# Two layers of a spatial-gating and attention mixer: the first queries of each attention turned later, and the second layer's first gating norm moved behind a GELU

## The chip, the cores and the metric

The kernel runs on one core of one Trainium2 chip. The metric is the device time of one execution in microseconds (us), lower is better. The time before is the median of three runs.

## The reference, cut to what matters

Two layers work on 256 latent tokens and 256 context tokens of width 2048, all in float32. Each layer normalises its input, scales and shifts it by a modulation computed from `c` and `c_ctx`, and multiplies it by one wide matrix whose columns are `u`, `v` and `za` of a gating branch and `q`, `k`, `v` and `zb` of an attention branch:

```python
u = gelu(u); v = rms_norm(gelu(v).reshape(b, n // 128, 128, 8, 128), v_norm_w)
s = einsum('gpq,bcqgd->bcpgd', w_sgu, v) + b_sgu.T[:, :, None]
sgu = u * s                                           # gating branch (SGU)
q = axial_rope(rms_norm(split_heads(q, 8), q_norm_w)) # 8 query heads, 2 key heads
p = softmax(einsum('bgrqd,bgkd->bgrqk', q, k) * 128 ** -0.5)
attn = einsum('bgrqk,bgkd->bgrqd', p, v)
y = concatenate([sgu * silu(za), attn * silu(zb)], -1) @ w_out
x = x + gate * y
```

In the first layer both token streams go through all of it; in the second the context gives only keys and values. Latent queries attend to all 512 keys, context queries to the 256 context keys.

## The kernel before, in words

Every matrix product is made of three float32r matmuls: an operand is split into a rounded high half (a copy on ScalarE, ACT) and the low half that is left (a subtraction on VectorE, DVE), and `three` multiplies high by high, low by high and high by low. L199 and L202 split a piece of weights (256 rows by 512 columns, a DMA of 512 KB into one of six `raw` buffers); `evac_split` (L474 and L475) splits what a transpose left in PSUM: keys `kT`, queries `qT`, probabilities `pt`.

The order of work on TensorE (PE), ACT, DVE and the DMA queue of SyncE (SP) is the order in which the Python program emits it, and each engine takes its own list in that order. The main stream (`Stream`) is a list of jobs, each a product with 512 weight columns. A job has eight pieces, and a piece has four **units** in the first layer (two or four in the second) of 1.3 to 1.5 us of matmuls each. After each unit `tick()` lets every waiting task emit its next step; tasks are taken in the order in which they were started, and a task's `yield n` means that it goes on n units later. `later(0, f)` emits f in the same tick, behind all older tasks.

Three tasks matter here.

- `attention_task`: it normalises and rotates keys and the first two blocks of queries, then turns (transposes on PE) the first queries (`turn_queries`, L519), splits them one unit later, and one unit after that begins its loop over heads (32 in the first layer, 16 in the second). A head's scores are in its first unit; its probabilities are turned one unit later and split one or two units after that, together with the next queries if the head is the second of its pair. `HEAD_PACE` makes a head three units long in the first layer and four in the second. No head begins while `zone[0]` is set, in the last piece of a job (four units in the first layer, two in the second). With the first head of each block of four another block's queries are normalised in the first layer (`Q_AT`), with the second in the second.
- `mod_rest`: the modulation rows that are needed later are computed as dot products on DVE (L283), two instructions a step in the first two parts and one in the last, a step every `MOD_PACE` units. It stands still while `hold[0]` is set; an attention sets it at its start and clears it just ahead of its first scores. While it stands still three `raw` buffers hold its rows.
- `head_norm` for the gating branch: after a tile's GELU has left PSUM (`sgu_v`, L659) four squares with sums on ACT (L440), a sum and a power (L427 on DVE, L428 on GpSimd, POOL), and the product (L452, DVE). `sgu_task` multiplies the tiles by the position matrices on PE (L685) `SGU_LAG` units after the job's end: 15 in the first layer, 6 in the second.

In this document h0, h1, ... are the heads of an attention. S0, S1, ... are the stream's units in the first layer from its first (32 to a job; S60 to S63 is the last piece of the job for the first half of `u`, and S64 begins the job for `za`). T1, T2, ... are the units of the second layer from the first after the key and value job: T1 to T16 is its first `v` job, T15 and T16 end its two tiles, and T17 begins the job for `u`. In the kernel before, the first layer's first queries are turned after S2, split after S3 and scored after S4; its heads begin after S4, S7, ..., S25, and then, behind each job's last piece, after S32, S35, ..., S59, and S64 and so on. In the second layer the same three steps come after T19, T20 and T21.

Lines of the helpers: L338 to L340 are the three matmuls of `three`, L533 the maximum of a head's scores on DVE, L536 its exponential on ACT, L641 the product of `u` with the gating sums on DVE, L543 the turn of the probabilities.

Of the kernel before, what the change touches and what calls it, by code (L numbers as in the profile page):

```python
# [31 lines left out]
QT_AT = 1  # L32
KEY_LAG = (3, 3)
Q_LAG = (0, 0)
NORM_PACE = (1, 1)
ACT_NORM = 'k'
ACT_SUM = 'kqs'
# [11 lines left out]
SGU_GAP = {4: 2, 2: 3}  # L49
# [3 lines left out]
WAVE = ((2, 6), 8, 10)  # L53
MOD_LOADS = ((4, 5, 6, 9), (2, 4, 6, 9))
AHEAD = {'raww': 3, 'rawm': 3}
MOD_PACE = (2.0, 1.6, 2.4)
PRE_HOLD = (True, True)
HEAD_PACE = (((1, 1, 1), (1, 1, 1), (1, 1, 1)), ((1, 2, 1),))
LAT = (0, 1)
# [3 lines left out]
def mixer_kernel(ctx: ExitStack, tc: tile.TileContext, a, out):  # L63
# [29 lines left out]
    def misc(s="ms"):  # L93
        return msp.tile([P, 512], F32, tag="ms", name=nm(s))
# [11 lines left out]
    def view(ap, pat, **kw):  # L106
        return ap.rearrange(pat, **kw)
# [202 lines left out]
    def spawn(gen, wait=0):  # L310
        tasks.append([gen, wait])
# [122 lines left out]
    def head_norm(q, n, kind):  # L434
# [3 lines left out]
        if kind in ACT_SUM:  # L438
            for h in range(n):
                S.activation(sq[:, h * HD:(h + 1) * HD], q[:, h, :], AF.Square, accum_out=ss[:, h:h + 1])  # L440
            yield NORM_PACE[0]
        else:
            S.activation(view(sq, "p (h d) -> p h d", h=n), q, AF.Square)
            yield NORM_PACE[0]
            V.tensor_reduce(out=ss, in_=view(sq, "p (h d) -> p h d", h=n), axis=AX.X, op=ALU.add)
        r = rstd_of(ss, n, HD)
        yield NORM_PACE[1]
        if kind in ACT_NORM:
# [28 lines left out]
    def attention_task(L, kv, qa, units, done):  # L477
# [20 lines left out]
        def query(u):  # L498
            hf, tt = u
            yield from norm_rope(L, "q", qa[hf][:, tt], 4, tt)  # L500
            yield Q_LAG[L["l"]]
            ready.add(u)
# [12 lines left out]
        def turn_queries(hf, tt, pr):  # L515
            assert (hf, tt) in ready
            ps = misc("qt")
            for i in range(2):
                T.transpose(out=ps[:, i * P:(i + 1) * P], in_=qa[hf][:, tt, 2 * pr + i, :], identity=ident)  # L519
            qT = t2([P, 2, 2, P], "qT", F32R)  # L520
            qT = [qT[:, 0], qT[:, 1]]
            return ps, qT
# [38 lines left out]

        while len(nk) < NT or units[0] not in ready:
            yield 1
        ps, qT = turn_queries(*pairs[0])
        yield 1
        evac_split(qT[0], qT[1], view(ps[:, :256], "p (h d) -> p h d", h=2))
        yield 1
        hold[0] = False
        paces = HEAD_PACE[L["l"]]
        n = len(heads)  # L570
# [84 lines left out]
    def sgu_v(L, buf, hf, nt):  # L655

        def f(tt, ps):
            b = buf[:, tt]
            S.activation(b, view(ps, "p (g d) -> p g d", g=4), AF.Gelu_apprx_tanh)  # L659
            spawn(head_norm(b, 4, "s"), SGU_GAP[nt] * tt)  # L660
        return f

    def sgu_consts(l, hf):
# [557 lines left out]
```

## Time and profile before

| what | before |
|---|---|
| median of 3 runs | 1194.63 us (1194.54 to 1194.81) |
| profiled execution, its own time | 1195.92 us |
| its span, first to last instruction | 1194.2 us |
| mean granted TensorE clock | 0.998 |
| PE busy, share of the span | 1163.5 us, 97% |
| DVE busy | 908.4 us, 76% |
| ACT busy | 521.8 us, 44% |
| DMA, mean over the span | 207 GB/s |

The profile is of one execution on the chip. A matmul's printed end is modelled and matmuls overlap: one of 512 columns is printed with 0.39 us and the next begins 0.23 us after it, one of 256 with 0.28 us and 0.12 us. So where the profile prints idle time ahead of a matmul, PE's issue stood still for 0.16 us longer than that.

### The profile page before, as it was taken

Reading aid. Unit: us, or ns where it says so; the run is one execution under the profiler, and the core shown is the slowest. Engines: PE = TensorE matmul, PEld = TensorE weight load, DVE = VectorE, ACT = ScalarE, POOL = GpSimd, SP = SyncE. Lnnn points to the kernel's source line nnn. Section 1 sums busy time; section 2 is a strip of 40 time slices with the busy share of each in tenths; the row PEclk is TensorE's granted clock in tenths of the full one; section 3 lists DMA queues with packets and bytes.
Section 4 is the critical chain, followed back from the end, with each engine's and each line's share of the span. In section 5 each row is a group of like instructions: output and inputs, shape, how many; then the busy total and the mean of one; then the engine's idle time right before and its main releaser. Section 6 shows DMA issues by size and latency. Waiting matters only on the chain.

```text
span 1194.2 us, 17949 instructions
## 1 busy us (share of the span) xinstructions
PE 1163.5 (97%) x6624; PEld 990.8 (83%) x6624; DVE 908.4 (76%) x1939; ACT 521.8 (44%) x992; POOL 46.9 (4%) x47
## 2 busy tenths in 40 slices
PE   4899999999999999999999999999999999999998
PEld 2567667888888888888888888987888989999998
DVE  5666769778888777989988998678558687767544
ACT  4422225565565432242232122246366777645332
POOL 0000002001000000010100000000011000000000
PEclk9999999999999999999999999999999999999999
DMA  9978672545354656676886765646456667677662
GB/s 319 372 269 303 243 267 96 158 138 181 108 160 141 191 182 208 203 233 217 264 282 211 228 200 186 229 124 218 135 164 197 218 195 222 206 260 249 223 204 89
DMA packets 131913, 247.52 MB, mean 207 GB/s; under 512 B 8641, under 2 KB 19425, under 8 KB 131825
## 3 DMA queue, kind: packets, MB, share of 16 engines
q1 hardware_dynamic: 130640, 242.08, 62.6%
q0 software_dynamic: 1184, 4.29, 1.1%
q8 instruction: 52, 0.85, 0.3%
q14 instruction: 37, 0.30, 0.1%
HBM read 244.23 MB, written 2.11 MB: 206 GB/s over the span
## 4 chain that ended last, share of the span: by engine, by line
PE 85%; DVE 6%; ACT 3%; DMA 3%; issue 1%; POOL 1%; SPq 1%; ACTq 0%; POOLq 0%; DVEq 0%
PE acc L338 25%; PE acc L340 25%; PE acc L339 25%; PE mod L231 2%; DVE lo L202 2%; DMA raw<-in_w_in 1%; DMA mod<-in_w_mod 1%; PE tp L543 1%; ACT hi L199 1%; PE sg L685 1%; DVE qa L872 1%; PE s L340 1%; PE o L339 1%; POOL rs L428 1%; PE o L340 1%
## 5 line engine op out<-in xcount | busy, mean ns | idle before, releaser
L199 ACT CAST hi<-raw 128x1024 fp32r<-128x1024 f32 (+1 forms) x242 | 250.7, 1036 | 399.8 <-PE acc L339 279.5
L202 DVE TENSOR_TENSOR lo<-raw,hi 128x1024 fp32r<-128x1024 f32 (+1 forms) x242 | 292.1, 1208 | 131.7 <-ACT hi L199 131.4
L283 DVE SCALAR_TENSOR_TENSOR junk<-raw,scb 128x512 f32<-128x512 f32 x448 | 308.0, 688 | 15.1 <-DMA raw<-in_w_modt 6.2
L338 PE MATMUL acc<-hh,hi 128*128 128x512 f32 x384 | 152.6, 397 | 0.0
L340 PE MATMUL acc<-hh,lo 128*128 128x512 f32 x384 | 149.8, 390 | 0.0
L339 PE MATMUL acc<-hl,hi 128*128 128x512 f32 x384 | 149.8, 390 | 0.0
L338 PE MATMUL acc<-hi,hh 128*128 128x512 f32 x320 | 130.2, 407 | 6.6 <-ACT hh L719 5.6
L340 PE MATMUL acc<-hi,hl 128*128 128x512 f32 x320 | 126.3, 395 | 0.1
L339 PE MATMUL acc<-lo,hh 128*128 128x512 f32 x320 | 126.3, 395 | 0.0
L338 PE MATMUL acc<-h,hi 128*128 128x256 f32 x384 | 110.3, 287 | 1.0 <-ACT s L659 1.0
L340 PE MATMUL acc<-h,lo 128*128 128x256 f32 x384 | 108.6, 283 | 0.0
L339 PE MATMUL acc<-h,hi 128*128 128x256 f32 x384 | 108.5, 283 | 0.0
L338 PE MATMUL acc<-mh,hi 128*128 128x512 f32 (+1 forms) x304 | 106.5, 350 | 0.0
L340 PE MATMUL acc<-mh,lo 128*128 128x512 f32 (+1 forms) x304 | 106.4, 350 | 0.0
L339 PE MATMUL acc<-ml,hi 128*128 128x512 f32 (+1 forms) x304 | 106.4, 350 | 0.0
L338 PEld LDWEIGHTS acc<-hi,hh 128*128 128x128 f32 x320 | 60.7, 190 | 32.3 <-issue 7.1
L340 PEld LDWEIGHTS acc<-hh,lo 128*128 128x128 f32 x384 | 72.1, 188 | 15.3
L339 PEld LDWEIGHTS acc<-hl,hi 128*128 128x128 f32 x384 | 72.3, 188 | 13.5
L338 PEld LDWEIGHTS acc<-hh,hi 128*128 128x128 f32 x384 | 72.2, 188 | 13.5
L428 POOL TENSOR_TENSOR rs<-rs,nhalf 128x4 f32<-128x4 f32 (+1 forms) x36 | 41.4, 1149 | 892.1 <-DVE rs L427 892.1
L339 PE MATMUL acc<-lo,h 128*128 128x512 f32 x192 | 75.3, 392 | 0.7 <-DVE lo L202 0.3
L338 PE MATMUL acc<-hi,h 128*128 128x512 f32 x192 | 75.7, 394 | 0.0
(163 smaller groups left out, 2158.0 us busy)
## 6 DMA issues: line engine op xcount, KB each, us to landing
raw<-in_w_in SPq DMA_DIRECT2D x173, 512.0 KB, 4.3
raw<-in_w_modt SPq DMA_DIRECT2D x128, 512.0 KB, 4.7
raw<-in_w_out SPq DMA_DIRECT2D x64, 512.0 KB, 5.0
mod<-in_w_mod SPq DMA_DIRECT2D x15, 1024.0 KB, 8.7
raw<-in_w_mod SPq DMA_DIRECT2D x30, 512.0 KB, 9.7
scb<-crow SPq DMA_DIRECT2D x12, 512.0 KB, 5.9
xT<-in_xT SPq DMA_DIRECT2D x8, 512.0 KB, 8.1
x<-in_xT POOLq DMA_DIRECT2D x4, 1024.0 KB, 11.0
```

The lines of the kernel that those rows point to most:

```text
L199: S.copy(hi, rs)
L202: V.tensor_tensor(out=lo, in0=rs, in1=hi.bitcast(F32), op=ALU.subtract)
L231: T.matmul(self.ps[j:j + 32, :wd], sc[:, k, :], self.raw[k], start=k < 4, stop=k >= KT - 4)
L283: V.scalar_tensor_tensor(out=junk, in0=rs[i][:, b_, :], scalar=1.0, in1=scbs[q][:, s_, :], op0=ALU.mult, op1=ALU.mult, accum_out=part[:, 2 ...
L338: T.matmul(ps, lhi, rhi, start=first, stop=False)
L339: T.matmul(ps, lhi, rlo, start=False, stop=False)
L340: T.matmul(ps, llo, rhi, start=False, stop=last)
L428: G.tensor_tensor(out=r, in0=r, in1=nhalf[:, :n], op=ALU.pow)
L543: T.transpose(out=tp[:, c * P:(c + 1) * P], in_=p_[:, c * P:(c + 1) * P], identity=ident)
L685: T.matmul(ps[:, tt * P:(tt + 1) * P], buf[:, tt, g, :], ws[:, g, :], start=True, stop=True)
L872: later(0, lambda: V.tensor_tensor(out=dst[:, tt], in0=ps, in1=dst[:, tt], op=ALU.add))
```

## The change

In both layers the attention waits two more units before it turns its first queries (`ENTRY`), and one unit more between their split and the first scores (`FIRST_LO`), so that the clearing of `hold[0]` and every head follow three units later than before, where the job's last piece doesn't stop them. In the second layer the norm of a `v` job's first tile starts two units later and that of the second one unit later (`SGU_AFTER`; for four tiles, the first layer, nothing changes). The three paces of `mod_rest` become 1.95, 1.55 and 2.3 units.

```diff
@@ -32,6 +32,9 @@
 Q_LAG = (0, 0)
+ENTRY = (2, 2)
+FIRST_LO = 1
+SGU_AFTER = {4: 0, 2: 2}
 NORM_PACE = (1, 1)
@@ -53,7 +56,7 @@
-MOD_PACE = (2.0, 1.6, 2.4)
+MOD_PACE = (1.95, 1.55, 2.3)
@@ -561,10 +564,11 @@
         while len(nk) < NT or units[0] not in ready:
             yield 1
+        yield ENTRY[L["l"]]
         ps, qT = turn_queries(*pairs[0])
         yield 1
         evac_split(qT[0], qT[1], view(ps[:, :256], "p (h d) -> p h d", h=2))
-        yield 1
+        yield 1 + FIRST_LO
         hold[0] = False
@@ -657,7 +661,7 @@
             S.activation(b, view(ps, "p (g d) -> p g d", g=4), AF.Gelu_apprx_tanh)
-            spawn(head_norm(b, 4, "s"), SGU_GAP[nt] * tt)
+            spawn(head_norm(b, 4, "s"), SGU_AFTER[nt] + (SGU_GAP[nt] - SGU_AFTER[nt] // 2) * tt)
         return f
```

## Rows read from the trace of the kernel before

**Rows 1.** The page, busy time: engine, us, share of the span, instructions.
```profile
PE 1163.5 (97%) x6624; PEld 990.8 (83%) x6624; DVE 908.4 (76%) x1939; ACT 521.8 (44%) x992; POOL 46.9 (4%) x47
```
**Rows 2.** Waits of PE: who, for whom, us in total, times, longest.
```profile
PE qt L519 <- DVE rs L427: 1.8, 1, 1.8
PE s L340 <- DVE qT L475: 1.4, 3, 0.8
PE acc L338 <- ACT s L659: 1.0, 1, 1.0
...
PE o L339 <- DVE pt L475: 0.3, 1, 0.3
```
**Rows 3.** Timeline, first layer's first queries: start, duration, engine, instruction [idle before].
```profile
206.19 0.69 DVE L471 TENSOR_TENSOR qa<-qa,sq 128x512 f32<-128x512 f32 x1
...
207.03 0.41 PE L519 MATMUL qt<-ident,qa 128*128 128x128 f32 x2 [1.78 <-DVE rs L427]
...
208.99 0.69 DVE L452 TENSOR_TENSOR qa<-qa,rs 128x512 f32<-128x512 f32 x1 [0.23 <-POOL rs L428]
...
210.39 0.42 DVE L475 TENSOR_TENSOR qT<-qt,qT 128x256 fp32r<-128x256 f32 x1
...
210.87 0.50 PE L340 MATMUL s<-kT,qT 128*128 128x512 f32 x1 [0.20 <-DVE qT L475]
...
212.65 1.21 DVE L202 TENSOR_TENSOR lo<-raw,hi 128x1024 fp32r<-128x1024 f32 x1
```
**Rows 4.** Timeline of PE, second layer's entry.
```profile
904.60 0.39 PE L338 MATMUL acc<-h,hi 128*128 128x256 f32 x1 [0.98 <-ACT s L659]
...
911.35 0.50 PE L340 MATMUL s<-kT,qT 128*128 128x512 f32 x1 [0.76 <-DVE qT L475]
...
914.57 0.61 PE L685 MATMUL sg<-ws,s 128*128 128x128 f32 x4
```
**Rows 5.** Timeline of ACT, the same stretch.
```profile
902.80 0.30 ACT L440 ACTIVATE sq<-s 128x128 f32<-128x128 f32 x1
...
903.97 0.58 ACT L659 ACTIVATE s<-acc 128x512 f32<-128x512 f32 x1
```
**Rows 6.** Timeline of DVE, the same stretch.
```profile
904.29 0.69 DVE L452 TENSOR_TENSOR qa<-qa,rs 128x512 f32<-128x512 f32 x1
...
912.55 0.69 DVE L452 TENSOR_TENSOR s<-s,rs 128x512 f32<-128x512 f32 x1
```
**Rows 7.** The power on POOL there: count, shortest, median, longest ns.
```profile
L428 POOL TENSOR_TENSOR rs<-rs,nhalf x4: 1006/1008/1424, 894.8 to 911.5; 128x4 f32<-128x4 f32 x4
```
**Rows 8.** Timelines of ACT, DVE and PE, first layer, S57 to S67.
```profile
311.58 0.30 ACT L440 ACTIVATE sq<-qa 128x128 f32<-128x128 f32 x1
...
315.19 0.69 DVE L533 TENSOR_REDUCE nmx<-s 128x1 f32<-128x512 f32 x1 [1.37 <-PE s L340]
...
317.65 1.28 ACT L636 ACT_TABLE_LOAD   x1
...
323.21 0.39 PE L338 MATMUL s<-kT,qT 128*128 128x512 f32 x1
...
327.31 0.68 DVE L533 TENSOR_REDUCE nmx<-s 128x1 f32<-128x512 f32 x1
...
328.43 0.39 PE L338 MATMUL s<-kT,qT 128*128 128x512 f32 x1
...
330.66 0.69 DVE L475 TENSOR_TENSOR pt<-tp,pt 128x512 fp32r<-128x512 f32 x1 [0.19 <-ACT pt L474]
```
**Rows 9.** Groups of DVE from 315.1 to 331.3: count, busy us, mean ns.
```profile
L283 DVE SCALAR_TENSOR_TENSOR junk<-raw,scb 128x512 f32<-128x512 f32 x8 | 5.5, 686 | 0.1
L641 DVE TENSOR_TENSOR s<-s,act 128x512 f32<-128x512 f32 x4 | 2.7, 684 | 0.0
```
**Rows 10.** Windows: stretch, length, busy time of PE, PEld, DVE, ACT, POOL, PEclk, DMA.
```profile
52.60:56.00 3.40, 1.32 (x6) 0.64 (x5) 3.22 (x8) 0.91 (x2) 0.00 (x0) 1.00 1.05 389
56.00:59.50 3.50, 3.50 (x10) 2.48 (x8) 3.32 (x7) 1.84 (x3) 0.00 (x0) 0.51 0.83 304
```

## Prediction

> **What bounds the kernel now.** I read the page's busy times first: PE works through 97% of the span, DVE through 76%, ACT through 44% [rows 1]. So time is to be had only where PE stands still. The list of PE's waits says where that is: behind the start of the program there are few places, and four of them belong to this change [rows 2]. The timelines then show what is late at each place; the share of DVE over the whole span hides that DVE is full at just these places. All idle times below are printed ones plus 0.16 us, because a matmul is printed 0.16 us longer than it holds up the next.
>
> **The entry of the first layer.** PE waits 1.78 us ahead of the first query turn, because the rotation of these queries (L471) begins on DVE only at 206.19, and 0.20 us more in the first scores for the split's low half [rows 3]. With 0.16 each that is 2.30 us. Two more units ahead of the turn are 2.7 us of matmuls, so the turn would be reached at 207.03 - 1.94 + 2.7 = 207.8, behind the rotation's end at 206.88: the first wait goes. What is late next is the split. Its low half now comes behind all that DVE has been given by then: the second block's product, its rotation, and a weight piece (L202) that before lay behind the scores. DVE's list doesn't move with PE there, because it waits only for the power that ends at 208.95. From the product at 208.99: product 0.7, two small products 0.7, rotation 0.7 and 0.6, weight piece 1.15, split 0.42, so 213.3 [rows 3]. PE reaches the third matmul of the scores at 207.8 + 3.0 (two units as before) + 1.4 (one more) + 0.46 = 212.7, and waits about 0.7. Gain: 2.30 - 0.72 = 1.6 us. Bounds: no new wait 2.3, a wait of 1.2 leaves 1.1.
>
> **The entry of the second layer.** Two waits [rows 4]: 0.98 for PSUM that a tile's GELU frees, 0.76 for the split; with 0.16 each 2.07 us. ACT does four squares of the first tile (902.80 on, 1.17 us for four) ahead of the second GELU at 903.97 [rows 5]. With the norm two units later this GELU begins at 902.80 and ends at 903.4, when PE wants the space (904.60 - 1.14 = 903.46): the first wait goes. Three more units hide the split. But the second tile's norm now comes one unit later, while PE is 2 us early. DVE from 904.29 [rows 6]: queries' product 0.6, weight piece 1.15, rotation 0.8, sum 0.1, rotation 1.4, first tile's product 0.65, weight piece 1.15, sum 0.1, weight piece 1.15, split 0.35, product of the second tile 0.7. That is 8.1 us, so 912.4, or 912.8 if a power takes 1.42 us and not 1.01 [rows 7]. The gating matmuls (L685), at 914.57 before [rows 4], would be reached at 914.57 - 2.07 - 0.8 (the scores now come behind them) = 911.7 and wait 0.7 to 1.2. I take 1.0; before, the product was over at 913.24 [rows 6], well ahead of them. Gain 1.1 us; bounds 0.3 and 2.07.
>
> **The heads behind the entry.** In the first layer seven heads and not eight fit ahead of S28, so behind each job's last piece another head of the pair stands: h7, h17 and h27 (second of a pair) after S32, S64 and S96, where h8, h18 and h28 (first) stood. A second head turns the next pair's queries, splits them one unit on, and the next scores need them one unit after that. The other waits in the trace go with this: one for a split at 274.8 (1.4 - 0.20 - 0.76 = 0.44 of the third row), one for a split of probabilities (0.3) [rows 2]. With 0.16 each 1.1 us.
>
> What comes in their place I worked out at S64. Before, DVE is full there: 15.5 us from the maximum after S59 (315.19) to the split after S66 (330.66), and the maximum of the scores after S64 (PE 323.21) is taken only at 327.31 [rows 8]. In the list are eight L283, four products of `u`, two weight pieces [rows 9], a rotation of queries whose squares begin at 311.58 [rows 8], and splits. It did no harm, because after S64 stood a first head: the queries of the next scores had been split ahead of the last piece. With a second head there, PE turns the next queries after S65, and their split after S66 is behind the whole list, with the scores of h18 one unit later, at about 328.7 (328.43 before [rows 8]). The list changes so: the query block belongs to h16, now after S59 and not S56, so its squares come behind the first GELU of the job's end, its product and rotation between the products of `u`. Less work by 0.8 us (no query split in between, narrower probabilities). More waits on DVE: weight piece 0.5 (ACT takes the exponential and the weights' high half 0.7 later), first product of `u` 0.75 (behind the ACT table load of 1.28 [rows 8]), probabilities 1.3 (their high half lies behind four squares and a GELU), the queries' product 0.65 (power 1.0 [rows 7]). From 315.9, where the maximum of h16 would begin: 15.5 - 0.8 + 3.2 = 17.9, so the split begins at 333.8 and ends at 334.2. The third matmul of h18's scores is due at 329.15: a wait of 5.0 us. Without any of the added waits it is 1.8. I take 4.4, since the two longest follow from ACT's order and the others may shrink.
>
> The same reckoning at S34 and S98, where no rotation or fewer sums fall into the list, leaves margins of a microsecond and more. In the second layer the queries of h6 and h14 are split right behind the last activations of a job too, but DVE has one L283 a step there and is not behind: margins of 0.2 to 0.3 us, for which I set 0.3 of loss in all, 0 to 1.
>
> **The rest.** The paces: 448 L283 as before. The first part has 64 steps, so it gains 3.2 units and starts two or three later: the sum is nothing, and around S57 to S67 its steps fall on the same units as before. The second part ends some 6 units earlier; nothing of PE waits for it [rows 2]. SP's queue: during the longer hold weights keep three of the six `raw` buffers, and each load, with all that is queued behind it on SP, waits for the L202 of the piece three earlier. By the lists above DVE's pieces come no later than before, so I cost this at nothing. If a piece were a unit late, one wait of up to 1.4 us would show at L338 behind a `lo`. No DMA is added.
>
> **Sum**, in the profiled execution (span 1194.2, its own time 1195.92, 1.29 above the median): -1.6 - 1.1 - 1.1 + 4.4 + 0.3 = +0.9 us. With 1.8 at S67 it is -1.7, with 5.0 +1.5. On the median 1194.63 that is 1195.5, own range 1192.9 to 1196.5. Other medians lie within 0.27 us, so 0.2% (2.4 us) is about the least that I call a difference.
>
> **Rivals.** (1) *Nothing new waits after S66*: DVE isn't that late, and the split is ready a unit after it is emitted. For it: in the trace queries turned behind a second head wait at only a few places [rows 2]. Against it: DVE's maximum after S64 lies 3.6 us behind PE [rows 8]. It decides below a wait of 1.1 us. Then -1.6 - 1.1 - 1.1 + 0.3 = -3.5 or, if also the gating matmuls don't wait, -4.5: 1190 to 1191.
>
> (2) *The wait after S66 slows PE's clock*, on the other side. Between 52.6 and 56.0 PE had 1.32 us of work, and in the next 3.5 us the granted clock was 0.51, the lower level (1.2 GHz of 2.4) [rows 10]. At half the rate such a stretch loses 1.7 us of work. With 5.0 us of standing at S67, broken only by two matmuls, the same can follow: +1.5 + 1.7 = 3.2, so 1197.8. It decides at a wait of about 4 us. Against it: the mean granted clock is 0.998 over the span, so the 1.94 us ahead of the first query turn had no such sequel.
> The Trainium skill, "TensorE: Matmul & The Clock Gate", section "Why this matters for your kernels", advises against gaps in TensorE's work amid a kernel for this reason: the clock falls back. By it a gap as at S67 would cost more than itself, +3.2 in place of +1.5; the dip in the trace agrees.
>
> (3) *The change doesn't do what it says*: DVE is the limit at both entries, and the waits only move. Then the gains are the lower bounds, 1.1 and 0.3: 1196.5 to 1198 with the wait at S67. I count it half to the forecast and half to (2).
>
> **Chances.** Forecast within 0.2%: 0.43. Rival (1), faster: 0.30. Slower, by (2) or the worse half of (3): 0.27. The range from 1190.6 to 1198.0 reaches into both.
>
> **What would show it.** Right: no idle PE ahead of L519 near 207; 0.5 to 1 us in the first scores; in the second layer no wait of L338 for L659, but one of about 1 us at the first L685 for L452; no wait of L340 for `qT` near 274; a wait of 3 to 5 us for `qT` in the scores after S67, near 330, with L470 and L641 ahead of the split on DVE. Wrong: if that wait is under 1 us, the kernel is faster and my order of DVE's list or its waits there are wrong; if PEclk falls near 335, rival (2).

## The result and the profile after

The changed kernel takes 1203.84 us (median of 4 runs, 1203.55 to 1204.18) against 1194.72 us of the kernel before in the same series: a ratio of 1.007, 95% interval 1.0058 to 1.0082, or 9.1 us more. The forecast was 1195.5 us with a range up to 1198.0, so the result lies 8 us over it and outside its range. The profiled execution took 1203.86 us, with a span of 1202.1 us, 7.9 us longer than that of before.

The page's busy times of the changed kernel look as before [rows 1]; the list of PE's waits doesn't (columns: us in total, times, longest):

```profile
PE 1166.9 (97%) x6624; PEld 992.4 (83%) x6624; DVE 909.8 (76%) x1939; ACT 521.5 (43%) x992; POOL 46.3 (4%) x47
```
```profile
PE s L341 <- ACT qT L477: 3.5, 1, 3.5
PE sg L689 <- DVE s L455: 1.6, 2, 0.9
PE s L343 <- DVE qT L478: 1.5, 2, 0.8
PE rsb L707 <- DVE dg L699: 1.5, 1, 1.5
PE acc L341 <- ACT sums L712: 1.2, 1, 1.2
PE o L342 <- DVE pt L478: 0.8, 1, 0.8
PE acc L341 <- ACT act L640: 0.5, 1, 0.5
```

The change's lines stand three or four further down: L341 to L343 are the three matmuls of a product (before L338 to L340), L477 and L478 the split's high and low half (before L474, L475), L286 the product of modulation rows (before L283), L205 the weight piece's low half (before L202), L689 the gating matmuls (before L685), L640 the activation of a gate (before L636).

Of the waits of before [rows 2], those ahead of the first query turn, of L338 for L659, and of L340 for `qT` near 274 are gone, as forecast. New is 3.5 us for `qT` in one piece, and what follows it. PE's timeline at that place, the scores of h18:

```profile
323.21 0.39 PE L343 MATMUL acc<-hh,lo 128*128 128x512 f32 x1
327.07 0.50 PE L341 MATMUL s<-kT,qT 128*128 128x512 f32 x1 [3.47 <-ACT qT L477]
327.41 0.55 PE L342 MATMUL s<-kT,qT 128*128 128x512 f32 x1
328.80 0.79 PE L343 MATMUL s<-kT,qT 128*128 128x512 f32 x1 [0.85 <-DVE qT L478]
329.39 0.63 PE L341 MATMUL acc<-hh,hi 128*128 128x512 f32 x1
329.82 0.63 PE L342 MATMUL acc<-hl,hi 128*128 128x512 f32 x1
...
334.43 0.39 PE L342 MATMUL acc<-hl,hi 128*128 128x512 f32 x1
```

Ahead of 323 and from 334.43 on, matmuls of 512 columns start 0.23 us apart, between 329.39 and 333.66 0.43 us. The table of windows (us; busy times; then PEclk, DMA share, GB/s) gives the granted clock there:

```profile
322.00:328.00 6.00, 2.48 (x9) 1.26 (x8) 5.90 (x12) 2.81 (x5) 0.00 (x0) 0.96 0.28 87
328.00:334.00 6.00, 5.20 (x14) 4.22 (x15) 4.97 (x12) 3.18 (x6) 0.00 (x0) 0.50 0.49 129
334.00:340.00 6.00, 6.00 (x34) 5.18 (x33) 3.72 (x11) 2.44 (x4) 0.00 (x0) 0.97 0.67 223
```

From 328 to 334 PE is busy for 5.20 of 6 us and does 14 matmuls where it does 34 in the next six: it is at the lower of its two levels (0.50). Busy time alone would hide this loss.

The queries of h18 had been turned on PE at 320.0. Their high half is copied by ACT in its own order, behind the exponential of h17, and that one stands 4.78 us for its maximum, which DVE gives only at 324.6; a table load of 1.28 us lies between the two. The low half comes on DVE at 328.33 (DVE's list is shown further down):

```profile
324.69 1.28 ACT L539 ACT_TABLE_LOAD   x1 [4.78 <-DVE nmx L536]
...
326.66 0.36 ACT L477 CAST qT<-qt 128x256 fp32r<-128x256 f32 x1
```

The other new waits, from PE's timeline: the first layer's entry, the output projection of the first layer (two), the second layer's entry, and the second v job of the second layer (two):

```profile
211.80 0.50 PE L343 MATMUL s<-kT,qT 128*128 128x512 f32 x1 [0.66 <-DVE qT L478]
...
657.64 0.47 PE L341 MATMUL acc<-mh,hi 128*128 128x512 f32 x1 [1.17 <-ACT sums L712]
659.56 0.47 PE L341 MATMUL acc<-mh,hi 128*128 128x512 f32 x1 [0.31 <-DVE x L969]
...
918.60 0.49 PE L689 MATMUL sg<-ws,s 128*128 128x128 f32 x2 [0.93 <-DVE s L455]
...
1008.38 0.39 PE L342 MATMUL o<-pt,vs 128*128 128x256 f32 x1 [0.83 <-DVE pt L478]
...
1013.23 0.49 PE L689 MATMUL sg<-ws,s 128*128 128x128 f32 x2 [0.70 <-DVE s L455]
```

To compare many runs I add up, from the matmul records, PE's **lost time**: the distance between two starts, less 0.227, 0.120 or 0.064 us for a matmul of 512, 256 or 128 columns, where more than 0.06 us is left. It counts standing and slow matmuls alike. By stretch of the span, in us (all runs of the study; the last two columns are the lost time behind 203 against before's, and the measured difference of the medians from the kernel before in the same series):

```
stretch (us)    203- 220- 315- 340- 640- 790- 895- 925- 995-  behind  meas-
                220  315  340  640  790  895  925  995  end   203     ured
before          2.9  2.3  1.3  1.4  0.5  3.5  2.8  0.8  0.8    0        0
after           1.1  1.6  7.9  1.6  2.5  4.0  2.1  1.8  3.3   +9.5    +9.1
f1_entry0       1.1  2.6  7.1  1.8  0.5  3.2  2.8  0.8  0.8   +4.5    +5.5
f2_entry1       2.7  2.3  1.3  1.4  0.9  3.4  3.0  2.2  0.8   +1.5    +2.2
f3_sgu          2.6  2.3  1.3  1.4  0.8  2.9  2.9  0.8  5.8   +4.5    +4.4
f4_pace         2.9  5.5  1.2  2.5  1.8  2.3  2.9  0.8  0.8   +4.6    +6.0
e1_entry0       1.2  2.5  7.2  1.8  0.4  3.3  1.8  4.3  6.5  +12.7   +13.6
e2_entry1       3.0  6.0  1.3  2.4  0.8  2.7  3.4  1.8  1.2   +6.4    +6.8
e3_sgu          2.7  2.8  1.3  1.4  0.9  2.8  1.6  5.9  3.9   +7.0    +7.5
e4_pace         2.8  6.0  1.2  2.3  2.5  2.7  2.1  6.6  4.9  +14.7   +14.4
e5_unflip       1.2  7.0  1.2  1.5  1.9  3.8  2.1  1.8  3.3   +7.5    +6.0
e6_oldpace      1.1  2.5  7.5  1.8  0.5  3.6  2.2  1.8  3.3   +7.9    +7.5
e7_fill         1.2  1.7  3.7  1.6  2.1  3.7  2.1  1.8  3.3   +4.8    +8.7
e9_mend         1.1  6.0  1.2  1.5  0.5  3.9  2.1  2.0  0.9   +2.9    +2.2
g11_two         1.4  7.5  0.3  1.7  0.5  3.6  2.9  0.8  0.8   +3.0    +1.5
g20_turn        2.6  7.4  0.3  1.8  0.5  3.0  2.9  0.8  0.8   +3.9    +4.3
h1_short        1.4  5.9  0.3  1.6  0.5  3.8  1.8  6.4  5.4  +10.8    +9.7
h2_mend         1.6  7.3  0.4  1.8  0.5  3.7  2.1  1.7  1.2   +4.0    +2.9
k1_hold         1.4  4.1  0.3  1.6  0.9  2.4  2.8  0.9  0.8   -1.1    -0.5
k2_hold         1.2  2.6  1.2  1.7  0.9  2.3  2.8  0.9  0.8   -1.9    -1.3
```

The table is of one execution of each kernel. Ahead of 203, where the program is the same in all, the sum lies anywhere from 34.3 to 36.6 from one execution to another, and a kernel's runs lie up to 5 us apart; so a tenth in this table tells a place, not a total. Its last two columns agree within 1.6 us for all kernels but e7_fill, which does 3.2 us more work.

### The profile page after: what moved, and what is told of

The parts are those of the page before. It is cut to its first block, busy times and chain, and to the rows that moved or that the text cites. A ratio compares the mean times of both kernels' runs of the same rounds, so it can differ in the third digit from the quotient of the medians.

```text
span 1202.1 us, 17955 instructions
## 1 busy us (share of the span) xinstructions
PE 1166.9 (97%) x6624; PEld 992.4 (83%) x6624; DVE 909.8 (76%) x1939; ACT 521.5 (43%) x992; POOL 46.3 (4%) x47
## 4 chain that ended last, share of the span: by engine, by line
PE 76%; DVE 11%; DMA 6%; issue 3%; ACT 3%; POOL 1%; SPq 1%; DVEq 0%; ACTq 0%; POOLq 0%
PE acc L341 23%; PE acc L343 22%; PE acc L342 22%; DVE junk L286 3%; DVE lo L205 3%; DMA raw<-in_w_modt 3%; PE mod L234 2%; DMA raw<-in_w_in 2%; DMA mod<-in_w_mod 1%; PE tp L546 1%; ACT hi L202 1%; POOL rs L431 1%; PE s L343 1%; PE o L343 1%; PE o L342 1%
## 5 line engine op out<-in xcount | busy, mean ns | idle before, releaser
L202 ACT CAST hi<-raw 128x1024 fp32r<-128x1024 f32 (+1 forms) x242 | 250.5, 1035 | 395.4 <-PE acc L342 266.6
L205 DVE TENSOR_TENSOR lo<-raw,hi 128x1024 fp32r<-128x1024 f32 (+1 forms) x242 | 292.6, 1209 | 135.4 <-ACT hi L202 134.7
L286 DVE SCALAR_TENSOR_TENSOR junk<-raw,scb 128x512 f32<-128x512 f32 x448 | 308.5, 689 | 16.2 <-DMA raw<-in_w_modt 7.2
L341 PE MATMUL acc<-hh,hi 128*128 128x512 f32 x384 | 153.7, 400 | 0.0
L343 PE MATMUL acc<-hh,lo 128*128 128x512 f32 x384 | 150.6, 392 | 0.0
L341 PE MATMUL acc<-hi,hh 128*128 128x512 f32 x320 | 129.8, 406 | 7.0 <-ACT hh L723 5.6
L343 PE MATMUL acc<-hi,hl 128*128 128x512 f32 x320 | 126.2, 394 | 0.1
L341 PE MATMUL acc<-h,hi 128*128 128x256 f32 x384 | 110.6, 288 | 0.5 <-ACT act L640 0.5
L343 PE MATMUL acc<-h,lo 128*128 128x256 f32 x384 | 108.6, 283 | 0.0
L341 PE MATMUL acc<-mh,hi 128*128 128x512 f32 (+1 forms) x304 | 106.8, 351 | 1.5 <-ACT sums L712 1.2
L343 PE MATMUL acc<-mh,lo 128*128 128x512 f32 (+1 forms) x304 | 106.5, 350 | 0.0
L341 PEld LDWEIGHTS acc<-hi,hh 128*128 128x128 f32 x320 | 60.6, 189 | 32.6 <-issue 7.1
L343 PEld LDWEIGHTS acc<-hh,lo 128*128 128x128 f32 x384 | 72.5, 189 | 15.6
L341 PEld LDWEIGHTS acc<-hh,hi 128*128 128x128 f32 x384 | 72.8, 190 | 13.5
L341 PE MATMUL acc<-hi,h 128*128 128x512 f32 x192 | 75.7, 394 | 0.0
```

Of the source, the lines that this page charges most:

```text
L202: S.copy(hi, rs)
L205: V.tensor_tensor(out=lo, in0=rs, in1=hi.bitcast(F32), op=ALU.subtract)
L286: V.scalar_tensor_tensor(out=junk, in0=rs[i][:, b_, :], scalar=1.0, in1=scbs[q][:, s_, :], op0=ALU.mult, op1=ALU.mult, accum_out=part[:, 2 ...
L341: T.matmul(ps, lhi, rhi, start=first, stop=False)
L343: T.matmul(ps, llo, rhi, start=False, stop=last)
```

## The experiments

### The four parts, each by itself

The change has four parts: the later entry in the first layer, in the second, the later norm, and the paces. The switches, against the changed kernel:

```
-ENTRY = (2, 2)
-FIRST_LO = 1
+ENTRY = (2, 0)        # f1_entry0; (0, 2) f2_entry1; (0, 0) f3_sgu, f4_pace
+FIRST_LO = (1, 0)     # (0, 1); (0, 0)
-SGU_AFTER = {4: 0, 2: 2}
+SGU_AFTER = {4: 0, 2: 0}          # f3_sgu keeps 2
-MOD_PACE = (1.95, 1.55, 2.3)
+MOD_PACE = (2.0, 1.6, 2.4)        # f2_entry1 (2.0, 1.6, 2.3); f4_pace keeps the new
-        yield ENTRY[L["l"]]
+        yield from [ENTRY[L["l"]]] * (ENTRY[L["l"]] > 0)
```

A first set had the switches set to 0 with the `yield` left as it is. In this program a task that pauses for 0 units still gives up one, so in these four the entry that was to stay came **one unit later**: in the second layer in e1_entry0, in the first in e2_entry1 (which has the new paces), in both in e3_sgu and e4_pace. Their expectations speak of kernels that didn't run; what they show is a shift by one unit.

> The kernel before with the later first queries in the first layer alone (ENTRY and FIRST_LO for layer 0; SGU_AFTER and MOD_PACE as before). Theory, the entry of the first layer is the cause: it gains some 2.5 us (1.8 at the entry, 0.6 at 274) and loses 6.6 at S64 to S70 (two stalls of the scores behind S67, 3.6 and 1.2 us, and matmuls 0.43 us apart for some 5 us after them), so +4 us, about 1198.7. Rival A, the new paces crowd DVE with products of the modulation rows ahead of S67: without them the scores behind S67 wait for at most 1 us, and the kernel gains 2 us or more, 1192.5 or less. Rival B, the stall is there but the slow matmuls came by chance in one profiled execution: +1.5 to +2.5 us, 1196 to 1197.

> The kernel before with the later first queries in the second layer alone, and the new MOD_PACE (SGU_AFTER as before, first layer's entry as before). Theory: the wait for the GELU's PSUM at the entry stays (1.0 us), that for the split goes (0.8 us); the head that stands behind each job changes its parity, which costs some 0.7 us at 937 and some at the second job of v (1007): together -0.5 to +1 us, 1194 to 1195.7, with what the paces do on top. Rival: the entry itself costs nothing and gains 0.8, and the waits at 937 and 1007 belong to the norm's shift: 1193.9 or less if the paces do nothing.

> The kernel before with SGU_AFTER alone. Theory: the wait of the second tile for the PSUM of its GELU (1.0 us) goes, and the first SGU matmul waits 1.1 us for the norm instead; at the second job of v, where no wait was, the same shift makes a new one of 0.9 us at 1012: +0.5 to +1.2 us, about 1195.5. Rival: the waits of the second job come from the head parity that the entry flips, and the shift alone leaves the second job without a wait: -0.3 to +0.2 us.

> The kernel before with the new MOD_PACE alone. Theory: the paces move the products of the modulation rows into the beginning of the first layer's output projection, where after has 1.96 us of stalls near 656 and 659 and before none: +1.5 to +2 us, 1196.2 to 1196.7. Rival: those stalls come from the later release of these products at the first layer's entry, which the new paces only half make up; then the paces alone end earlier and nothing changes: -0.3 to +0.3 us, 1194.4 to 1195.

Measured: 1.0112 (1.0098 to 1.0126), 1.0054 (1.0042 to 1.0067), 1.0061 (1.0049 to 1.0074), 1.0120 (1.0104 to 1.0135). In the three with the second layer's entry one unit later the lost time from 925 on is 9.8 to 11.5 us (before 1.6; the change itself, three units later, 5.1). A small shift there is dearer than a large one; the heads take four units each, and the waits that come are those of jobs for their own activations (L640, L663), up to 2.3 and 1.7 us at a time. With both switches truly off:

> The kernel before with the later first queries in the first layer alone, this time with every other switch truly off: the second layer's entry, the norm and the paces are those of before. Theory, the first layer's entry makes the stall of the scores behind S67: it gains 1.7 us at the entry, and loses 6 us between 315 and 340 (3.6 us for the high half of qT, 0.9 to 1.2 for the low half, and slow matmuls behind them), 1198.5 to 1199.5. The run with the second layer's entry one unit later (e1_entry0) was at +13.6 us; by this theory the other 9 us are the second layer's and go. Rival: part of those 9 us comes from the products of the modulation rows, which the later entry shifts through the whole first layer; then this kernel stays above 1202.

> The kernel before with the later first queries in the second layer alone; the last of the three paces is 2.3 (it must be, so that the gates of the second layer are there in time), the others are those of before. Theory: the wait for the split at the entry goes (0.8 us), that for the GELU's PSUM stays, 0.7 us of new wait at 937, and some tenths at 1007: -0.3 to +0.8 us, 1194.5 to 1195.5. Rival, the parity of the heads behind the second job costs as much as a shift by one unit did (ACT's activations of the heads meet the job's GELUs and SILUs: waits of 1 to 2 us at 936, 968, 1003 and 1037): +4 us or more.

> The kernel before with SGU_AFTER alone, with both entries truly as before. Theory: 1.0 us of wait for the GELU's PSUM goes and 0.9 to 1.1 us at the first SGU matmul comes; the same at the second job, where nothing was to gain, adds 0.9: +0.5 to +1.2 us, about 1195.6. Rival: the stalls of the second job belong to the entry's shift; the norm alone moves nothing, -0.3 to +0.2 us.

> The kernel before with the new paces alone, with both entries truly as before. Theory: with the entry one unit later the same paces had 2.6 us of stall at 273 and 1.6 at 700, which a kernel with the paces of before (e3_sgu) had not; so by themselves they cost +1 to +3 us, 1195.8 to 1198. Rival: both stalls need the later entry too, and the paces alone change nothing: -0.3 to +0.3 us.

Measured: **f1_entry0** 1.0045 (1.0032 to 1.0058), +5.5 us, half a microsecond over what the theory gave: by place 1.8 gained at the entry, 5.8 lost from 315 to 340. **f2_entry1** 1.0016 (1.0007 to 1.0025), +2.2 us, over the range expected: 1.4 lost from 925 to 995, and at the entry, where the wait for the split is gone, 1.1 us for the load of the SGU's weights. **f3_sgu** 1.0036 (1.0023 to 1.0048), +4.4 us where about 0.9 was expected. The entry of the second layer gains nothing by the norm alone (2.9 against 2.8); the second v job loses 5.0. PE's timeline and the windows there, in f3_sgu:

```profile
1008.64 0.49 PE L689 MATMUL sg<-ws,s 128*128 128x128 f32 x2 [2.05 <-DVE s L455]
```
```profile
1002.00:1008.00 6.00, 4.01 (x31) 3.78 (x31) 3.83 (x11) 4.71 (x14) 1.01 (x1) 1.00 0.40 132
1008.00:1014.00 6.00, 5.36 (x31) 5.36 (x32) 3.38 (x7) 1.86 (x3) 0.00 (x0) 0.72 0.75 262
```

The gating matmuls stand for the second tile's product, which the shift put a unit later, and the clock falls behind them. **f4_pace** 1.0048 (1.0036 to 1.0061), +6.0 us where 1 to 3 were expected. The paces are no small matter: at 274 the wait for the split's low half, 0.6 us before, is 2.4, and the clock falls with it. DVE's list and PE in f4_pace (two products of the modulation rows, L286, stand ahead of the third gating tile's norm, the weight piece and the split; before, they came behind the split):

```profile
273.41 0.69 DVE L286 SCALAR_TENSOR_TENSOR junk<-raw,scb 128x512 f32<-128x512 f32 x1
...
274.13 0.69 DVE L286 SCALAR_TENSOR_TENSOR junk<-raw,scb 128x512 f32<-128x512 f32 x1
...
274.75 0.69 DVE L455 TENSOR_TENSOR s<-s,rs 128x512 f32<-128x512 f32 x1
275.36 1.22 DVE L205 TENSOR_TENSOR lo<-raw,hi 128x1024 fp32r<-128x1024 f32 x1
276.49 0.41 DVE L478 TENSOR_TENSOR qT<-qt,qT 128x256 fp32r<-128x256 f32 x1
```
```profile
276.96 0.39 PE L343 MATMUL s<-kT,qT 128*128 128x256 f32 x1 [2.21 <-DVE qT L478]
```

The four alone come to 5.5 + 2.2 + 4.4 + 6.0 = 18.1 us, together to 9.1. They aren't separate: with the first layer's later entry the heads at 274 stand elsewhere and the paces do no harm there, and with the second layer's later entry the norm's loss at the second v job is 2.4 and not 5.0.

### Undoing one thing in the changed kernel

e5_unflip:
```
-            while ZONE[0] and zone[0] and j < n:
+            while ZONE[0] and zone[0] and j < n and (L["l"], j) != (0, 7):
```
e6_oldpace:
```
-MOD_PACE = (1.95, 1.55, 2.3)
+MOD_PACE = (2.0, 1.6, 2.3)
```
e7_fill:
```
-                live[j] = scores(hf, tt, qT, i)
+                live[j] = scores(hf, tt, qT, i, 14 if (L["l"], j) == (0, 18) else 0)
...
-        def scores(hf, tt, qT, i):
+        def scores(hf, tt, qT, i, fill):
...
             s_ = misc("s")[:, :n]
+            for _ in range(fill):
+                T.matmul(s_, kT[:, 0, hf, :P], kT[:, 0, hf, k0:], start=True, stop=True)
```
e9_mend: the edits of e5_unflip and e6_oldpace, and
```
-            spawn(head_norm(b, 4, "s"), SGU_AFTER[nt] + (SGU_GAP[nt] - SGU_AFTER[nt] // 2) * tt)
+            spawn(head_norm(b, 4, "s"), SGU_AFTER[nt] * (1 - hf) + (SGU_GAP[nt] - SGU_AFTER[nt] * (1 - hf) // 2) * tt)
```

> The changed kernel, but its head h7 of the first layer need not wait for the end of the job's last piece, so that again eight heads stand ahead of that job's end and behind every later one stands the first head of a pair, as in the kernel before. Theory, the parity of the heads behind a job's end makes the stall behind S67: without it 4.8 us of standing and some 2 us of slow matmuls between 315 and 340 go, -5 to -7 us against the changed kernel, 1197 to 1199. Rival: DVE is behind there in any case since the later entry shifts its list; a wait of 3 us or more stays in that stretch and the time stays above 1201.

> The changed kernel with the first two paces of before (2.0 and 1.6; the third stays 2.3). Theory: the first two paces alone made the stalls in the first layer's output projection (2.0 us near 656 here, 1.3 us near 701 with the paces alone), so these go: -1.5 to -2.5 us, 1201.3 to 1202.3. Rival: as the paces alone cost 5.8 us, of which 3.2 at 274 where the later entry has taken the wait away already, they are a help in this kernel at another place: 0 or a loss, 1203.8 or more.

> The changed kernel with 14 more matmuls (128x512, into the PSUM tile that the scores of h18 overwrite afterwards, output unchanged) ahead of the scores that stand still at 323: 14 x 0.227 = 3.2 us of work inside a stall of 3.6 us. Theory, PE's standing lowers its clock and the slow matmuls that follow are the price: the stall shrinks to 0.4 us plus the 1.2 for the low half, matmuls of 0.43 us don't appear, and although PE has 3.2 us more to do the kernel is 1.5 to 2.5 us faster than the changed one, 1201.3 to 1202.3. Rival: the matmuls behind the stall are slow for another reason (operands or PSUM that DVE and ACT hold up): the time stays within 0.5 us of the changed kernel or rises.

> The changed kernel with three mendings: the parity of the heads kept as in the run e5_unflip, the first two paces of before, and the norm's shift in the second layer for the first v job alone (not for the second, where alone it cost 5 us). If the three losses are separate: 1203.8 - 6 (parity) - 2 (paces) - 2.4 (second v job) = 1193.4, and it beats the kernel before by about 1 us. Rival: each mending shifts the list of the engine that is full at the next place, as the four parts of the change did by themselves (+5.4, +1.9, +4.3 and +5.8 us, together 17 and not 9): then it stays at 1196 or above.

**e5_unflip**: 1201.21 us, 1.0053 (1.0040 to 1.0066). Half right: from 315 to 340 the 7.9 us are 1.2 again, so the place of the heads decides whether the stall stands there. But 5.4 us of it come back between 220 and 315, behind the first job's end (1.22 and 0.34 for `pt`, 0.89 for `qT`, and a granted clock of 0.80 from 268 to 274). **e6_oldpace**: 1202.78, 1.0061 (1.0048 to 1.0074): the 2 us near 656 go, as expected, and 0.9 come at 275. So the waits in the output projection are the paces': with them L286 fills DVE where the first results of that projection are to be taken.

**e7_fill**: 1203.99, 1.0078 (1.0065 to 1.0091): no gain, yet not for the rival's reason.

```profile
328.52 3.47 PE L535 MATMUL s<-kT 128*128 128x512 f32 x14 [3.21 <-ACT p L541]
331.83 0.39 PE L341 MATMUL s<-kT,qT 128*128 128x512 f32 x1
...
332.28 0.39 PE L343 MATMUL s<-kT,qT 128*128 128x512 f32 x1
```
```profile
322.00:328.00 6.00, 3.32 (x17) 2.45 (x15) 5.93 (x13) 1.59 (x2) 0.00 (x0) 1.00 0.29 87
328.00:334.00 6.00, 5.48 (x25) 4.50 (x26) 4.38 (x11) 2.77 (x7) 0.00 (x0) 1.00 0.30 87
```

The fillers had to wait themselves, 3.2 us, for the PSUM tile that the head before still needed for its exponential (L541 is that line here): two things were late at once. Then 3.2 us of work ran that isn't in the changed kernel, the split was ready by its end, and in this execution no slow matmul followed: 3.7 us lost from 315 to 340 in place of 7.9. The 4.2 us that this saves are the 1.2 us wait for the low half, the slow matmuls, and a first stand 0.3 us shorter; taking the two waits from the difference, **the fall of the clock cost 4.2 - 1.2 - 0.3 = 2.7 us**.

**e9_mend**: 1197.41, 1.0020 (1.0011 to 1.0028): the rival. The second v job is as before (0.9) and the output projection too, but the 6.0 us from 220 to 315 stay.

### Is it the third unit?

In the first layer the change comes three units later, and one head takes three. Counted in the program, eight heads stand ahead of the first job's end before, and with one or two units more; with three, seven. So with two units the heads behind the end stay as they were:

```
+ENTRY = (1, 0)        # g20_turn (2, 0), h1_short (1, 0), h2_mend (1, 2)
+FIRST_LO = (1, 0)     # g20_turn (0, 0), h1_short (1, 1), h2_mend (1, 1)
```
All else is as in f1_entry0; h1_short and h2_mend have a last pace of 2.3, and h2_mend the norm's shift for the first v job, as e9_mend.

> The kernel before with the first layer's first queries turned one unit later and their first scores one more: two units in place of the three of the change; all else as before. Eight heads still stand ahead of the job's end (the eighth two units later than before), so the first head of a pair stands behind it, as before. Theory, the third unit is what flips the heads and makes the stall behind S67: the turn waits 0.55 us and the low half of the first scores some 0.5 us, 1.1 to 1.4 us in place of 2.9 at the entry; 315 to 340 stays as before: -0.5 to -1.8 us, 1193 to 1194.5. Rival: eight heads two units later crowd the job's end as the three units later did in e5_unflip (7.0 us between 220 and 315, with the clock down): +2 us or more.

> The kernel before with the first layer's first queries turned two units later and the first scores right behind them as before; all else as before. Also two units, with the eight heads ahead of the job's end. Theory: the turn doesn't wait, but the split is given to DVE as late as in the change while the scores come a unit earlier, so the wait for the low half is 0.8 + 1.36 = 2.2 us: nothing is gained at the entry, and nothing lost between 315 and 340: -0.3 to +0.8 us. Rival: the split is ready earlier than that, and the gain is 1 us or more, as in g11_two.

> As g11_two, and in the second layer the first scores alone come one unit later (the turn and the norm as before; last pace 2.3). Theory: with 0.9 us less of wait for the split at the second layer's entry, and the wait for the GELU's PSUM left, it is 0.3 to 0.9 us under g11_two, 1192.3 to 1194. Rival: a shift by one unit there, as in the three runs with the second layer's entry one unit later, puts ACT's activations of the heads on the job's GELUs and SILUs (waits of 1 to 2 us at 936, 968, 1003 and 1037): +6 us or more.

> The run e9_mend with the first layer's entry of g11_two in place of its own (so the second layer has the change's entry, the norm's shift for the first v job alone, and a last pace of 2.3). Theory: the 4 us that e9_mend loses between 262 and 276 go with the third unit, and the second layer is a balance of small gains and losses (+0.5 us): 1193 to 1195. Rival: that loss stays, 1197.

Measured: g11_two 1197.19, 1.0015 (1.0006 to 1.0024); g20_turn 1200.01, 1.0036 (1.0024 to 1.0049); h1_short 1205.44, 1.0083 (1.0070 to 1.0097); h2_mend 1198.59, 1.0023 (1.0014 to 1.0032). Three go with their rivals or near them, and g20_turn is dearer than either theory had it: without the third unit a loss of much the same size stands at the first job's end, so the third unit decides where it stands and not whether there is one. The entry gains what was expected (1.4 in place of 2.9 with g11_two, 0.3 with g20_turn), and from 315 to 340 even 1 us is gained, but between 220 and 315 7.5 and 7.4 us are lost in place of 2.3, with one stand of 2.6 us for the split's low half (up to 274.9 and 277.6) and a fall of the clock behind it (0.72 from 274 to 280 in g11_two). h1_short shows again what one unit does in the second layer.

So neither the parity nor the third unit explains the stalls; whatever the heads' place, one job's end or another had one. What all of them have on DVE ahead of the late split is the products of the modulation rows.

### The products taken out of DVE's list

DVE in the changed kernel, from 317 to the split for which h18's scores wait:

```profile
317.10 0.67 DVE L286 SCALAR_TENSOR_TENSOR junk<-raw,scb 128x512 f32<-128x512 f32 x1
...
317.81 0.69 DVE L286 SCALAR_TENSOR_TENSOR junk<-raw,scb 128x512 f32<-128x512 f32 x1
...
320.09 0.69 DVE L455 TENSOR_TENSOR qa<-qa,rs 128x512 f32<-128x512 f32 x1 [0.90 <-POOL rs L431]
...
321.30 0.69 DVE L286 SCALAR_TENSOR_TENSOR junk<-raw,scb 128x512 f32<-128x512 f32 x1
...
323.92 0.69 DVE L536 TENSOR_REDUCE nmx<-s 128x1 f32<-128x512 f32 x1
...
325.85 1.22 DVE L205 TENSOR_TENSOR lo<-raw,hi 128x1024 fp32r<-128x1024 f32 x1
326.98 0.68 DVE L286 SCALAR_TENSOR_TENSOR junk<-raw,scb 128x512 f32<-128x512 f32 x1
327.71 0.69 DVE L286 SCALAR_TENSOR_TENSOR junk<-raw,scb 128x512 f32<-128x512 f32 x1
...
328.33 0.42 DVE L478 TENSOR_TENSOR qT<-qt,qT 128x256 fp32r<-128x256 f32 x1
```

Six of them (the fourth, at 322.03, is not shown) take 6 x 0.69 = 4.1 us between 317 and 328, and no step of the heads needs them. Four lie ahead of h17's maximum (323.92), on which the high half hangs, all six ahead of the low half. In the last two runs they are held back there, and the heads stay where they are:

```
-            nq = tp = None
+            nq = tp = None; hold[0] = L["l"] == 0 and j in (8, 9)     # k1_hold: g11_two; k2_hold: f1_entry0 with (15, 16, 17)
...
+MOD_PACE = (2.0, 1.6, 2.3)
```

> As g11_two (first layer's first queries one unit later, first scores one more), and the products of the modulation rows (L286) are held back while the two heads h8 and h9 behind the first job's end begin (last pace 2.3, so that the gates are there in time). In g11_two the low half of a split waits at 272 behind two pairs of these products (4 x 0.69 = 2.8 us of DVE), PE stands 2.59 us for it and its clock falls. Theory, these products make that stall: it is 0 to 1.2 us, the clock stays up, and 2.5 to 4 us go against g11_two, so that the gain at the entry is seen: 1192 to 1194.5, at or under the kernel before. Rival: the list of DVE there is set by the power (POOL) and by the pieces of weights that ACT gives late; the split comes no more than 0.7 us earlier and the time stays within 1 us of g11_two.

> As f1_entry0 (the first layer's entry of the change alone, three units), and the products of the modulation rows (L286) are held back while the heads h15 to h17 behind the end of the u job begin. In f1_entry0 the scores of h18 stand 3.6 and 0.9 us for the two halves of qT, with six of these products (4.1 us) in DVE's list between 319 and 331. Theory, DVE's list is the cause, so the stall shrinks to less than 1 us, the clock stays up, and 5 to 6 us of the 5.4 that f1_entry0 lost go: 1193 to 1196. Rival: what is late is the turn of queries after the rotation, which waits for ACT's squares and POOL's power: the stall keeps 2.5 us or more and the time stays above 1198.

**k1_hold**: 1194.93 us, 0.9996 (0.9987 to 1.0005), 2.0 us under g11_two when each is taken against its own series and a little less than the theory's 2.5 to 4: the stand that begins at 272 is 0.70 us (2.43 in g11_two), the clock stays at 1.00 from 268 to 280. **k2_hold**: 1194.14 us, 0.9991 (0.9982 to 1.0000), 1.3 us under the kernel before and 6.8 under f1_entry0, taken in the same way. DVE, PE and the windows in k2_hold, at the scores that stood for 3.6 and 0.9 us in f1_entry0:

```profile
325.70 1.22 DVE L205 TENSOR_TENSOR lo<-raw,hi 128x1024 fp32r<-128x1024 f32 x1
326.84 0.42 DVE L478 TENSOR_TENSOR qT<-qt,qT 128x256 fp32r<-128x256 f32 x1
```
```profile
326.22 0.39 PE L342 MATMUL s<-kT,qT 128*128 128x512 f32 x1
327.31 0.50 PE L343 MATMUL s<-kT,qT 128*128 128x512 f32 x1 [0.70 <-DVE qT L478]
```
```profile
322.00:328.00 6.00, 5.30 (x30) 4.27 (x29) 5.97 (x12) 3.27 (x6) 0.00 (x0) 1.00 0.01 1
328.00:334.00 6.00, 6.00 (x30) 4.97 (x29) 5.16 (x13) 3.81 (x7) 0.00 (x0) 1.00 0.69 192
```

The wait for the high half is gone, that for the low half keeps 0.70 us behind the weight piece, and the clock stays up. DVE's order from 312 to the split is that of f1_entry0 in all but the products. The last pace of 2.3, which both runs have besides, isn't what does it: e6_oldpace and h1_short have it too and keep their stands of 3.6 and 2.6 us. The change's own entry then gives back what it promised: 1.7 us at the entry and nothing lost behind it. The interval of k2_hold reaches to 1.0000, so that it beats the kernel before is likely and not certain; no run in this study is clearly faster.

## Why the prediction was wrong, step by step

**The entry of the first layer** was right: PE stood 0.66 us in the first scores, with the 0.16 0.82 (0.72 taken; the working's own times, 213.3 and 212.7, give 0.6), and the lost time there fell by 1.8 us (1.6 forecast). f1_entry0 has the same.

**The entry of the second layer** was right in its mechanism: both waits of before [rows 4] are gone, and the gating matmuls wait for the second tile's product, 0.93 us (with the 0.16 about 1.1; 1.0 taken). Its gain is 0.7 us (1.1 taken, bounds 0.3 and 2.07).

**The other waits** went as forecast: 0.7 us at 274. That for the probabilities near 330 can't be told apart, since the stall took its place.

**The wait at S67** was right in cause and size and nearly in place: 3.63 + 1.17 = 4.8 us of standing (4.4 taken, 1.8 to 5.0 bounded), with the rotation (L473, L470 before) and L645 ahead of the split. DVE's list took 17.9 us from h16's maximum (310.39) to the split (328.33), as reckoned. Two things about it differ. The larger part was the wait for the high half, ahead of the first matmul and not the third, because ACT makes that half behind h17's exponential; as the low half came last all the same, the sum stays. And it came at 323 to 329, where the text had about 329 to 334: 3.4 us of that are the gains ahead of it and a shorter program start, 0.9 us the matmuls of the one head fewer that stands ahead of it, and the rest stays open. The step that failed here is the decision between the forecast and rival (2). I set the fall of the clock as a rival that decides "at a wait of about 4 us", and I expected 4.4, so by my own rule it belonged in the sum; what I put against it was one stand of 1.94 us at the entry that had no sequel, and a mean clock of 0.998 over the span, which can't tell: it is 0.997 in the changed kernel, where the clock fell. The fall cost 2.7 us (1.7 taken for rival 2), and it followed this stand in all four profiled kernels that have it (3.63 us in the changed one, e1_entry0 and e6_oldpace, 3.62 in f1_entry0). The Trainium skill, "TensorE: Matmul & The Clock Gate", section "Why this matters for your kernels", warns of just this, and here the trace agrees: 1.00 from 316 to 322, ahead of the stand, 0.50 behind it. That of e7_fill doesn't (last section). Together the stretch lost 6.6 us more than before, where the sum had 4.4, less the 0.5 us for the probabilities.

**The paces** were costed at nothing, "nothing of PE waits for it". That is the second failed step. I asked who waits for the products, and not who stands behind them on DVE: 2.0 us near 656, shown by e6_oldpace; by themselves they cost 6.0 us (f4_pace). "around S57 to S67 its steps fall on the same units as before" was good enough there (e6_oldpace and f1_entry0, with the old paces, have the same stand) and said nothing of the 300 us behind.

**The second v job of the second layer** was left out. The norm's shift acts on both v jobs; I worked out the first, where it takes a wait away, and not the second, where no wait was and 2.4 us came. f3_sgu shows it (5.0 us by itself) and e9_mend takes it away (0.9, as before). This is a missing term, not one mis-sized.

**The job ends of the second layer** were taken at 0.3 us (0 to 1): 1.1 us from 925 to 995, most of it one wait of 0.5 us for the activation at 937. Mis-sized.

The terms as measured, in lost time: -1.8 (entry), -0.7 (274), +6.6 (315 to 340), +0.2 (to 640), +2.0 (output projection), +0.4 (790 to 895, where the one wait of L707 for L699 is 0.7 longer; over the runs it is printed with anything from nothing to 1.5 us, and why stays open), -0.7 (second entry), +1.1 (job ends), +2.4 (second v job): +9.5 us, while the medians differ by 9.1. Without the fall of the clock, the paces and the second v job it would have been 9.5 - 2.7 - 2.0 - 2.4 = +2.4, where the forecast's sum had +0.9. The upper end of its own range, 1196.5, isn't that of its sum either: 1194.63 + 1.5 is 1196.1.

**What the experiments corrected in my own explanation.** After the result I held the flipped parity of the heads for the cause. It decides where the stall stands, but in e5_unflip, g11_two and g20_turn a stall came at the first job's end instead. The cause that held is DVE's list at a job's end, filled with products that nobody there needs: k1_hold and k2_hold take them out and leave the heads where they are, and at both places the stall shrinks to 0.7 us and no slow matmuls follow. Both run without the second layer's part of the change; that the same holds in the changed kernel itself was not tried. Why a shift by one unit in the second layer costs some 8 us was not tried further; the waits (for the activations of jobs, L640 and L663) are read from the trace alone.

## What to carry to other kernels

On a schedule written out by hand every shift of one part changes the phase of all that runs beside it: for each moved step go to all places where it happens (both layers, both jobs, every job's end), and for each engine near full there write its list anew. Work that nobody awaits costs what stands behind it on its engine; holding it back at the tight places was worth more here than moving the heads. If a forecast stand is as long as one after which the clock is seen to fall, put the slow matmuls into the sum, with their chance.

## What was not expected of the hardware

The length of a stand alone didn't tell whether the clock falls. It stayed at 1.00 behind one of 3.2 us (e7_fill, above) and behind the 1.8 us ahead of the first query turn in the kernel before ([rows 3]; 1.00 from 204 to 214); it fell behind stands of 2.2 us (f4_pace) and 2.05 us (f3_sgu, above) and behind the two of the changed kernel. The windows of f4_pace, where the stand ends at 276.96:

```profile
268.00:274.00 6.00, 6.00 (x37) 5.32 (x36) 5.06 (x13) 4.47 (x17) 1.98 (x2) 1.00 0.85 259
274.00:280.00 6.00, 3.79 (x15) 2.93 (x14) 5.14 (x15) 2.60 (x13) 0.57 (x1) 0.80 0.35 113
```

In f4_pace PE had been busy for all of the six microseconds ahead; so it had in e7_fill from 316 to 322. Nor does the schedule decide it. Up to 400 us PE, DVE, ACT and POOL have the same instructions in the same order in g11_two and h1_short; both stand 2.43 us for the same low half, up to 274.9 and 274.6, and the clock fell in the first and not in the second. The windows, of g11_two and then of h1_short:

```profile
274.00:280.00 6.00, 5.07 (x17) 4.02 (x18) 4.70 (x14) 3.98 (x15) 1.01 (x1) 0.72 0.80 249
```
```profile
274.00:280.00 6.00, 5.35 (x26) 4.51 (x27) 4.67 (x16) 4.12 (x15) 1.01 (x1) 1.00 0.75 253
```

Between 220 and 315 they lost 7.5 and 5.9 us, so this fall cost some 1.6. What makes the difference stays open; one execution of a kernel can't tell whether a stand will be followed by a fall in the next.

Also not expected: a task's shift by one unit (1.4 us) in the second layer cost nearly as much (about 8 us: h1_short against g11_two, e1_entry0 against f1_entry0) as the whole change did.
